# Short-conv adaLN layer in fp32: the turn of all tokens moved into the front as products with a diagonal of 1/rms

## The chip, the core and the metric

The kernel runs on one core of one Trainium2 chip. The metric is the device time of one execution in microseconds (us). The engines in this text are TensorE (PE, with its weight loads shown apart as PEld), VectorE (DVE), ScalarE (ACT) and the SyncE queue (SP), which issues nearly all of the DMAs. PSUM is the memory that PE writes; its tiles here come from two pools of buffers, "mm" (three buffers of two banks) and "sm" (two of one bank).

## The reference

One layer is computed for 256 tokens of width D = 2048, with inner width E = 4096:

```python
h = x / sqrt(mean(x*x) + eps) * g
shift, scale, gate = split(silu(c) @ ada_w + ada_b)     # ada_w is 2048 x 6144
h = h * (1 + scale) + shift
b, cg, v, gg = split(h @ w_in)                          # w_in is 2048 x 16384
u = causal_conv3(cg * v);  y = b * u * silu(gg)
x = x + gate * (y @ w_out);  out = rmsnorm(x, final_g)
```

All data are fp32. The weights are 128 MB (w_in), 48 MB (ada_w) and 32 MB (w_out), and each is read once.

## The kernel before, in words

A product with fp32 weights is made of three products in a faster format: `split` (L320) casts a piece of weights to `hi` on ACT (L324) and subtracts on DVE to get `lo` (L325), and PE multiplies hi by h's hi, hi by h's lo, and lo by h's hi (`product`, L419). Such a product needs h with the features on the partitions, so x is turned on PE first (`turn_x`, L281): ACT scales 512 columns of both token tiles by 1/rms (L285, L289), PE transposes them in blocks of 128 x 128 (L294), and ACT copies them out of PSUM into `xs` (L295). `modulate` (L300) then makes the hi and lo halves of `hT` for one pair of the 16 feature blocks, as soon as that pair's shift and scale are known.

Shift and scale come from ada_w. Two feature blocks at a time make a group: its 16 rows of blocks are multiplied by silu(c) and added up on DVE (`gv0` in the front, L348 and L350; `gv` later, L399 and L401), and PE or ACT adds over the partitions. In the front, three of the 16 blocks (7, 11, 15) are summed on PE instead (`sum0`, L337, products of one column), and a last such step adds `gv0`. So the front runs: load x (four DMAs), load ada_w's first columns (`at0`, twelve DMAs), square sums (ACT for token tile 0, L261; DVE for tile 1, L264), 1/rms (L270 to L272), the turn of the first 512 columns, the sums, `modulate(0, 2)`, first product. Between them, `idle(n)` (L238) puts n transposes of the identity on PE that nobody reads; the counts stand in `IDLE`. Everything of the front is pinned to the written order on each engine.

After the front, `plan()` lists steps: ("mm", ...) multiplies a chunk of 512 columns of w_in by the feature blocks that are ready, and ("ada", ...) loads one piece of a later group. An ada piece is two DMAs of 256 KB into one of four `at` buffers and two additions `gv` on DVE. A chunk's weights come as `raw_s`, 512 KB or 1 MB a DMA, in one of three `raw` buffers. The steps' order is fixed by the plan, but the order in which the pieces' instructions stand on SP, DVE and ACT is the scheduler's: it places them by priority and by its own estimate of when each could run. DVE works in its order: a `lo` behind a `gv` waits for that gv's DMA. The turns of the feature blocks 4 to 15 are put behind the 4th, 7th and 10th chunk (`LATER`, L486), with the turn of the convolution's taps (`rows2` into `cw`). SP's DMAs take eight semaphores in turn, so at most eight are under way, and a DMA into a buffer waits for DVE's last read of it.

After the "mm" chunks follow the second half of w_in (mm_b), the gates, and the product with w_out (mm_o).

Of the kernel before, what the change touches and what calls it, by code (L numbers as in the profile page):

```python
# [8 lines left out]
F32 = mybir.dt.float32  # L9
# [108 lines left out]
def short_conv_layer(ctx: ExitStack, tc: tile.TileContext, x, c, norm_g, ada_w, ada_b, w_in, conv_w, w_out, final_g, out):  # L118
# [69 lines left out]
    IDLE = (16, 30, 24, 14, 14, 6)  # L188
# [14 lines left out]
    for n, (j, kk) in enumerate(((0, 4), (4, 4), (8, 4), (12, 2), (14, 1), (15, 1))):  # L203
        at = wpool.tile([P, SLOT], F32, tag=("lo", "hi")[n % 2], name="at0", bufs=3)[:, : kk * 2 * NK0 * P]
        at = at.rearrange("p (k s f) -> p k s f", k=kk, s=2)
        if n == 0:
            wpool.tile([P, 32], F32, tag="line3", name="line3", bufs=1)
        if j == KT - 1:
            raw0 = raw_tile("raw0")
            first_load(raw0, 0)  # L210
        for s in range(2):
            nc.sync.dma_start(at[:, :, s, :], adas[:, j : j + kk, s, 0 : NK0 * P])  # L212
        first_ada.extend(at[:, i] for i in range(kk))
    for k in range(1, NK0):
        first_load(raw0, k)
# [20 lines left out]
    tp_idle = psum.tile([P, CT, T], F32, tag="mm", name="tp_idle")  # L236

    def idle(n):  # L238
        for _ in range(n):
            nc.tensor.transpose(tp_idle[:, 0, 0:P], ident, ident)  # L240

# [5 lines left out]
    idle(IDLE[0])  # L247
# [4 lines left out]
    idle(IDLE[1])  # L252
# [5 lines left out]
    for t in range(TT):  # L258
        for dh in range(2):
            if t == 0:  # L260
                sq = nc.scalar.activation(junk[:, t], xt[t][dh], AF.Square, accum_out=ssq[:, dh, t : t + 1])  # L261
                tc.add_manual_dep(sq.ins, root.ins.name, after, reason="one change of table")
            else:
                nc.vector.scalar_tensor_tensor(  # L264
                    out=junk[:, t], in0=xt[t][dh], scalar=1.0, in1=xt[t][dh], op0=ALU.mult, op1=ALU.mult,
                    accum_out=ssq[:, dh, t : t + 1],
                )
    nc.vector.tensor_copy(vec, tp_v)
    nc.vector.tensor_scalar_add(b_scale1, vec[:, 32:48], 1.0)
    nc.vector.tensor_tensor(out=rstd, in0=ssq[:, 0, :], in1=ssq[:, 1, :], op=ALU.add)  # L270
    nc.scalar.activation(rstd, rstd, AF.Sqrt, bias=eps_t, scale=1.0 / D)
    nc.vector.reciprocal(rstd, rstd)  # L272

# [5 lines left out]
    xs = [slot([P, CT, T], f"xs{j}") for j in range(KT // CT)]  # L279

    def turn_x(k0, k1, vector=False):  # L281

        c0, n = k0 % 8 * P, (k1 - k0) * P
        x0, x1 = (xt[t][k0 // 8][:, c0 : c0 + n] for t in range(TT))
        nc.scalar.activation(x0, x0, AF.Copy, scale=rstd[:, 0:1])  # L285
        if vector:
            nc.vector.tensor_scalar_mul(x1, x1, rstd[:, 1:2])
        else:
            nc.scalar.activation(x1, x1, AF.Copy, scale=rstd[:, 1:2])  # L289
        for i in range(0, k1 - k0, 2):  # L290
            tp = psum.tile([P, 2, T], F32, tag="sm", name="tp_x", bufs=2)
            for j in range(2):
                for t, xn in enumerate((x0, x1)):
                    nc.tensor.transpose(tp[:, j, t * P : (t + 1) * P], xn[:, (i + j) * P : (i + j + 1) * P], ident)  # L294
            nc.scalar.copy(xs[k0 // CT][:, k0 % CT + i : k0 % CT + i + 2, :], tp)  # L295
# [4 lines left out]
    def modulate(k0, nk, sums):  # L300

        ks = slice(k0, k0 + nk)
        if nk == 1:
            nc.vector.tensor_scalar(
                out=scale[:, ks], in0=sums[1], scalar1=b_scale1[:, ks], scalar2=gT[:, ks], op0=ALU.add, op1=ALU.mult
            )
            nc.scalar.activation(shift[:, ks], sums[0], AF.Identity, bias=b_shift[:, ks])
        else:
            nc.vector.tensor_tensor(out=scale[:, ks], in0=sums[1], in1=b_scale1[:, ks], op=ALU.add)
            nc.vector.tensor_tensor(out=scale[:, ks], in0=scale[:, ks], in1=gT[:, ks], op=ALU.mult)  # L310
            nc.vector.tensor_tensor(out=shift[:, ks], in0=sums[0], in1=b_shift[:, ks], op=ALU.add)
        for k in range(k0, k0 + nk):
# [19 lines left out]
    turn_x(0, 4)  # L332
# [8 lines left out]

    for k in range(KT):
        c_k = silu_c[:, k : k + 1]
        if k in ON_PE:
            idle(IDLE[2 + ON_PE.index(k)])
# [6 lines left out]
    pieces0 = [split(raw0[:, 0 : CT * P], CT * P)]  # L352
    modulate(0, NK0, (sums0[:, 0:NK0], sums0[:, NK0 : 2 * NK0]))
    idle(IDLE[-1])
# [131 lines left out]
    LATER = (4, 7, 10)  # L486
    whole = [0] * NCH
    for kind, *step in plan():
        if kind == "ada":
            ada_piece(*step)  # L490
        else:
            ch, k1 = step[0], step[3]
            part(*step)
            if step[2] == 0 and len(acc) in LATER:
                k = 4 + 4 * LATER.index(len(acc))
                with tc.issue_after(last_mm[0].ins), behind(ended):
                    turn_x(k, k + 4)
                    if k == 4:
                        turn(rows2, 0, 96, cw)
# [206 lines left out]
```

## Time and profile before

| what | us |
|---|---|
| time, median of 3 runs (all: 926.06, 925.84, 923.97) | 925.84 |
| span of the profiled execution | 925.9 |
| first product of the layer (L419) starts | 26.50 |
| PE's waits for `lo` behind it, three in number | 6.7 |
| PE busy in the span | 904.4 |
| DVE busy in the span | 613.9 |
| ACT busy in the span | 472.8 |

The profiled execution has no time of its own beside its span; 925.9 is within 0.1 us of the median. A row of the timeline gives start, duration, engine, line, operation, out<-in and the count of merged instructions, and in brackets the engine's idle time before it with what ended it. A row of windows gives, behind the stretch's bounds and length, the busy time and count for PE, PEld, DVE, ACT and POOL, then the granted PE clock (1.00 is full), the share of the DMA engines and GB/s. PE durations overlap, so the pace of a run of equal instructions is its length through its count.

### The profile page before, as it was taken

The page shows a single profiled execution, that of the slowest core. Times are in us where ns is not written, and L with a number is a line of the kernel's source. Part 1 is how long each engine was busy: PE and PEld are TensorE (multiplying, and loading weights), DVE is VectorE, ACT ScalarE, POOL GpSimd, SP SyncE. Part 2 cuts the span into 40 slices and gives each one's busy share as a digit, 9 for nine tenths or more (in the row PEclk, how much of TensorE's full clock was granted, in tenths as well). Part 3 has the DMA queues.
Part 4 walks back from the last instruction along what each step waited for, and adds up shares of the span by engine and source line. Part 5 has one row for each costly group of instructions (what it writes and reads, how often), then busy time and mean ns, then how long its engine had stood idle before and what let it go on. Part 6 is the DMA issues. An engine that isn't in the chain of part 4 may idle for free.

```text
span 925.9 us, 16464 instructions
## 1 busy us (share of the span) xinstructions
PE 904.4 (98%) x7119; PEld 869.6 (94%) x7119; DVE 613.9 (66%) x604; ACT 472.8 (51%) x465; POOL 0.7 (0%) x6
## 2 busy tenths in 40 slices
PE   7999899999999999999999999999999999999996
PEld 6999899999999999999999999999999988888885
DVE  5889888898486799875554455445554544545882
ACT  3787776675557856644434433443334433444333
POOL 0000000000000000000000000000000000000000
PEclk9999999999999999999999999999999999999999
DMA  9999999999895789776655665666556496566542
GB/s 314 355 367 355 367 329 338 350 365 358 268 306 186 219 297 357 243 231 201 202 186 188 199 204 184 189 199 204 183 183 195 140 348 226 186 200 205 182 137 92
DMA packets 163753, 227.66 MB, mean 246 GB/s; under 512 B 5680, under 2 KB 104160, under 8 KB 163296
## 3 DMA queue, kind: packets, MB, share of 16 engines
q1 hardware_dynamic: 163440, 226.51, 74.0%
q8 instruction: 56, 0.92, 0.4%
q14 instruction: 17, 0.14, 0.0%
q10 hardware_dynamic: 240, 0.09, 0.0%
HBM read 224.49 MB, written 2.10 MB: 245 GB/s over the span
## 4 chain that ended last, share of the span: by engine, by line
PE 88%; DMA 6%; DVE 3%; issue 1%; SPq 1%; ACT 1%; ACTq 0%; DVEq 0%
PE mm_b L419 38%; PE mm_s L419 31%; PE mm_o L604 6%; PE mm_o L605 6%; PE mm_o L603 6%; DMA at<-in_ada_w_dram 3%; DMA raw_s<-in_sc_w_in_dram 2%; DVE gv L401 1%; DVE lo L325 1%; DMA x<-in_x_dram 1%; SPq L212 0%; ACT hi L324 0%; PE ps_gate L542 0%; PE tp_g L408 0%; SPq L388 0%
## 5 line engine op out<-in xcount | busy, mean ns | idle before, releaser
L419 PE MATMUL mm_s<-hT,hi 128*128 128x256 f32 x2048 | 352.9, 278 | 0.1
L419 PE MATMUL mm_b<-hT,hi 128*128 128x256 f32 x2048 | 348.8, 276 | 0.0
L419 PEld LDWEIGHTS mm_s<-hT,hi 128*128 128x128 f32 x2048 | 310.4, 189 | 1.2 <-issue 0.5
L419 PEld LDWEIGHTS mm_b<-hT,hi 128*128 128x128 f32 x2048 | 308.4, 188 | 0.2 <-issue 0.2
L419 PE MATMUL mm_s<-hT,lo 128*128 128x256 f32 x1024 | 284.4, 279 | 6.8 <-DVE lo L325 6.7
L419 PE MATMUL mm_b<-hT,lo 128*128 128x256 f32 x1024 | 282.6, 276 | 0.0
L325 DVE TENSOR_TENSOR lo<-raw,hi 128x2048 fp32r<-128x2048 f32 (+1 forms) x66 | 148.1, 2244 | 135.1 <-ACT hi L324 135.1
L324 ACT CAST hi<-raw 128x2048 fp32r<-128x2048 f32 (+1 forms) x66 | 123.7, 1874 | 208.5 <-PE mm_b L419 150.2
L419 PEld LDWEIGHTS mm_s<-hT,lo 128*128 128x128 f32 x1024 | 193.1, 189 | 7.6 <-DVE lo L325 7.6
L419 PEld LDWEIGHTS mm_b<-hT,lo 128*128 128x128 f32 x1024 | 192.2, 188 | 0.2 <-issue 0.2
L325 DVE TENSOR_TENSOR lo<-raw_s,hi 128x2048 fp32r<-128x2048 f32 (+1 forms) x80 | 147.9, 1849 | 40.5 <-ACT hi L324 39.7
L324 ACT CAST hi<-raw_s 128x2048 fp32r<-128x2048 f32 (+1 forms) x80 | 124.6, 1557 | 67.6 <-PE mm_s L419 49.8
L325 DVE TENSOR_TENSOR lo<-raw_o,hi 128x2048 fp32r<-128x2048 f32 x32 | 73.3, 2291 | 65.1 <-ACT hi L324 65.0
L324 ACT CAST hi<-raw_o 128x2048 fp32r<-128x2048 f32 x32 | 61.0, 1907 | 107.2 <-PE mm_o L605 85.0
L604 PE MATMUL mm_o<-lo,y 128*128 128x512 f32 x256 | 99.7, 391 | 0.0
L603 PE MATMUL mm_o<-hi,y 128*128 128x512 f32 x256 | 99.3, 389 | 0.0
L605 PE MATMUL mm_o<-hi,y 128*128 128x512 f32 x256 | 99.3, 389 | 0.0
L401 DVE SCALAR_TENSOR_TENSOR gv<-at,silu_c,gv 128x512 f32<-128x512 f32 x105 | 78.6, 749 | 9.2 <-DMA at<-in_ada_w_dram 7.8
L440 ACT COPY acc<-mm_s 128x1024 f32<-128x1024 f32 x54 | 54.4, 1010 | 35.1 <-PE mm_s L419 34.9
L605 PEld LDWEIGHTS mm_o<-hi,y 128*128 128x128 f32 x256 | 48.0, 188 | 10.1 <-issue 0.2
L604 PEld LDWEIGHTS mm_o<-lo,y 128*128 128x128 f32 x256 | 48.0, 188 | 10.1 <-issue 0.2
L603 PEld LDWEIGHTS mm_o<-hi,y 128*128 128x128 f32 x256 | 48.0, 188 | 10.0
(94 smaller groups left out, 375.4 us busy)
## 6 DMA issues: line engine op xcount, KB each, us to landing
raw<-in_sc_w_in_dram SPq DMA_DIRECT2D x64, 1024.0 KB, 5.7
raw_s<-in_sc_w_in_dram SPq DMA_DIRECT2D x47, 1024.0 KB, 7.8
raw_o<-in_sc_w_out_dram SPq DMA_DIRECT2D x32, 1024.0 KB, 5.2
at<-in_ada_w_dram SPq DMA_DIRECT2D x114, 256.0 KB, 7.3
raw_s<-in_sc_w_in_dram SPq DMA_DIRECT2D x33, 512.0 KB, 5.8
at_g<-in_ada_w_dram SPq DMA_DIRECT2D x32, 512.0 KB, 8.0
at<-in_ada_w_dram SPq DMA_DIRECT2D x6, 512.0 KB, 8.8
x<-in_x_dram SPq DMA_DIRECT2D x4, 512.0 KB, 6.1
```

What stands on the lines that cost most here:

```text
L324: nc.scalar.copy(hi[:, :n], raw[:, :n])
L325: nc.vector.tensor_tensor(out=lo[:, :n], in0=raw[:, :n], in1=hi[:, :n].bitcast(F32), op=ALU.subtract)
L401: nc.vector.scalar_tensor_tensor(out=gv, in0=at4[:, i], scalar=c_k, in1=gv, op0=ALU.mult, op1=ALU.add)
L419: mm = last_mm[0] = nc.tensor.matmul(dst, w, h[:, k], start=begins and left, stop=ends, skip_group_check=True)
L440: nc.scalar.copy(acc[ch, q], bank)
L603: nc.tensor.matmul(po, yh, hi[:, o], start=opens, stop=False, skip_group_check=True)
L604: nc.tensor.matmul(po, yh, lo[:, o], start=False, stop=False, skip_group_check=True)
L605: nc.tensor.matmul(po, yl, hi[:, o], start=False, stop=ct == NCT - 1, skip_group_check=True)
```

## The change

All 16 feature blocks of both token tiles are turned in the front. No scaling of x on ACT and no transposes are left: a block of x is the stationary operand of a plain fp32 product, and the moving operand is `rooted`, the identity times 1/rms (128 x 128, made on DVE), so that the product both turns and scales. 1/rms is found for each token tile by itself (`root_of`): tile 0 by two squares on ACT, tile 1 by one on ACT and one on DVE. The results go into three "mm" buffers in PSUM, which ACT copies to `xs` 1024 columns at a time, and a fourth that takes the first one's buffer again. The turn of `rows2` moves into the front, between the two token tiles.

On SP the first half of the first weights (`raw0`) moves behind the last of `at0`. Of `gv0`'s blocks, five instead of three are summed on PE (7, 10, 11, 13, 15). The split of `raw0`'s first half on ACT and DVE moves behind shift and scale, within `modulate`. `IDLE` has 9 entries with other counts. Behind the front, the plan's steps are the same, without `LATER`.

```diff
-    IDLE = (16, 30, 24, 14, 14, 6)
+    IDLE = (16, 4, 4, 2, 8, 0, 0, 0, 5)
...
-        if j == KT - 1:
-            raw0 = raw_tile("raw0")
-            first_load(raw0, 0)
...
-    for k in range(1, NK0):
+    raw0 = raw_tile("raw0")
+    for k in range(NK0):
         first_load(raw0, k)
...
+    def root_of(t):
+        r = rstd[:, t : t + 1]
+        nc.vector.tensor_tensor(out=r, in0=ssq[:, 0, t : t + 1], in1=ssq[:, 1, t : t + 1], op=ALU.add)
+        nc.scalar.activation(r, r, AF.Sqrt, bias=eps_t, scale=1.0 / D)
+        nc.vector.reciprocal(r, r)
+        nc.vector.tensor_scalar_mul(rooted[:, t], ident, r)
+
+    def turn_x(tp, j, t):
+        for i in range(CT):
+            k = j * CT + i
+            nc.tensor.matmul(
+                tp[:, i, t * P : (t + 1) * P], xt[t][k // 8][:, k % 8 * P : (k % 8 + 1) * P], rooted[:, t],
+                start=True, stop=True, skip_group_check=True,
+            )
+
+    squares(0, 0, False)
+    squares(0, 1, False)
+    root_of(0)
+    nc.vector.tensor_copy(vec, tp_v)
+    nc.vector.tensor_scalar_add(b_scale1, vec[:, 32:48], 1.0)
+    for j in range(3):
+        turn_x(turned[j], j, 0)
+    turn(rows2, 0, 96, cw)
+    squares(1, 0, False)
+    squares(1, 1, True)
+    root_of(1)
+    idle(IDLE[2], turned[2])
+    for j in range(3):
+        turn_x(turned[j], j, 1)
+        nc.scalar.copy(xs[j], turned[j])
...
-    ON_PE = (7, 11, 15)
+    ON_PE = (7, 10, 11, 13, 15)
...
-    LATER = (4, 7, 10)
...
-            if step[2] == 0 and len(acc) in LATER:
-                k = 4 + 4 * LATER.index(len(acc))
-                with tc.issue_after(last_mm[0].ins), behind(ended):
-                    turn_x(k, k + 4)
-                    if k == 4:
-                        turn(rows2, 0, 96, cw)
```

The order on three places. First DVE in the front, before, from the square sums to the first of `gv0` (x10 and x11 are the halves of token tile 1, at0_96 the first piece of ada_w):

```order
L264 SCALAR_TENSOR_TENSOR junk_187,ssq_185<-x10_86 128x1024
L264 SCALAR_TENSOR_TENSOR junk_187,ssq_185<-x11_87 128x1024
L268 COPY vec_127<-tp_v_152 128x64
L269 TENSOR_SCALAR b_scale1_154<-vec_127 128x16
L270 TENSOR_TENSOR rstd_186<-ssq_185 128x2
L272 RECIPROCAL rstd_186<-rstd_186 128x2
L348 TENSOR_SCALAR gv0_205<-at0_96,silu_c_129 128x512
```

The same stretch of DVE with the change:

```order
L273 TENSOR_TENSOR rstd_162<-ssq_161 128x1
L275 RECIPROCAL rstd_162<-rstd_162 128x1
L276 TENSOR_SCALAR rooted_169<-ident_118,rstd_162 128x128
L289 COPY vec_127<-tp_v_154 128x64
L290 TENSOR_SCALAR b_scale1_156<-vec_127 128x16
L230 COPY cw_128<-tp_v_190 128x96
L263 SCALAR_TENSOR_TENSOR junk_163,ssq_161<-x11_87 128x1024
L273 TENSOR_TENSOR rstd_162<-ssq_161 128x1
L275 RECIPROCAL rstd_162<-rstd_162 128x1
L276 TENSOR_SCALAR rooted_169<-ident_118,rstd_162 128x128
L361 TENSOR_SCALAR gv0_221<-at0_96,silu_c_129 128x512
```

The copy of `cw`, which waits for PE's turn of `rows2`, now stands ahead of the squares of x11, and with them ahead of the second root and of all of `gv0`.

Second, PE in the front, before, from the turn's end to the layer's first product (tp_idle are the transposes that nobody reads):

```order
L240 MATMUL tp_idle<-ident 128x128 x24
L337 MATMUL sum_204<-silu_c,at_100 128x1 x4
L240 MATMUL tp_idle<-ident 128x128 x14
L337 MATMUL sum_204<-silu_c,at_103 128x1 x4
L240 MATMUL tp_idle<-ident 128x128 x14
L337 MATMUL sum_204<-silu_c,at_112 128x1 x4
L337 MATMUL sum_204<-ones,gv_205 128x1 x4
L240 MATMUL tp_idle<-ident 128x128 x6
```

The same stretch of PE with the change, from the products of token tile 1 on (x_86 and x_87 are its halves, x_85 is the second half of tile 0):

```order
L281 MATMUL tp_x<-rooted,x_86 128x128 x8
L281 MATMUL tp_x<-rooted,x_87 128x128 x4
L281 MATMUL tp_x<-rooted,x_85 128x128 x4
L281 MATMUL tp_x<-rooted,x_87 128x128 x4
L238 MATMUL tp_idle<-ident 128x128 x2
L347 MATMUL sum_220<-silu_c,at_100 128x1 x4
L238 MATMUL tp_idle<-ident 128x128 x8
L347 MATMUL sum_220<-silu_c,at_103 128x1 x8
L347 MATMUL sum_220<-silu_c,at_106 128x1 x4
L347 MATMUL sum_220<-silu_c,at_112 128x1 x4
L347 MATMUL sum_220<-ones,gv_221 128x1 x4
L238 MATMUL tp_idle<-ident 128x128 x5
```

Ahead of the sums now stand 20 products of token tile 1 and of the last 512 columns, and between the last four sums no transposes.

Third, DVE some 70 us behind the front, before, from the 20th to the 21st `lo` of raw_s (at_1593, at_1685 and at_1690 are the 25th to 27th ada piece; on SP, raw_s_1255 is issued ahead of at_1690):

```order
L325 TENSOR_TENSOR lo_1225<-raw_s_1222,hi_1224 128x1024
L401 SCALAR_TENSOR_TENSOR gv_1592<-at_1593,silu_c_129,gv_1592 128x512
L401 SCALAR_TENSOR_TENSOR gv_1592<-at_1685,silu_c_129,gv_1592 128x512 x2
L401 SCALAR_TENSOR_TENSOR gv_1592<-at_1690,silu_c_129,gv_1592 128x512 x2
L325 TENSOR_TENSOR lo_1258<-raw_s_1255,hi_1257 128x2048
```

The same two `lo` with the change (at_1442, at_1524 and at_1616 are the 24th to 26th piece; on SP, raw_s_1186 is issued ahead of at_1616):

```order
L334 TENSOR_TENSOR lo_1156<-raw_s_1153,hi_1155 128x1024
L413 SCALAR_TENSOR_TENSOR gv_1145<-at_1442,silu_c_129,gv_1145 128x512
L413 SCALAR_TENSOR_TENSOR gv_1523<-at_1524,silu_c_129,gv_1523 128x512
L413 SCALAR_TENSOR_TENSOR gv_1145<-at_1442,silu_c_129,gv_1145 128x512
L413 SCALAR_TENSOR_TENSOR gv_1523<-at_1616,silu_c_129,gv_1523 128x512
L334 TENSOR_TENSOR lo_1189<-raw_s_1186,hi_1188 128x2048
```

The 21st `lo` now stands behind one addition of the 26th piece, where it stood behind both additions of the 27th.

More of the change, by code (lines that the diff above doesn't have):

```diff
@@ L233, in turn, with idle @@
         return tp
-    tp_idle = psum.tile([P, CT, T], F32, tag="mm", name="tp_idle")
-    def idle(n):
+    turned = [psum.tile([P, CT, T], F32, tag="mm", name="tp_x") for _ in range(3)]
+    def idle(n, where):
         for _ in range(n):
-            nc.tensor.transpose(tp_idle[:, 0, 0:P], ident, ident)
+            nc.tensor.transpose(where[:, CT - 1, P:T], ident, ident)
     warm = const.tile([P, 1], F32, tag="warm", name="warm")
@@ L257, in short_conv_layer @@
     junk = hpool.tile([P, TT, HX], F32, tag="big", name="junk")
[L258 to L272, printed above, removed]
     hT = hpool.tile([P, KT, 2 * T], F32R, tag="big", name="hT")
@@ L279, in short_conv_layer, with squares @@
     xs = [slot([P, CT, T], f"xs{j}") for j in range(KT // CT)]
[L281 to L285, printed above, removed]
+    rooted = slot([P, TT, P], "rooted")
+    def squares(t, dh, vector):
         if vector:
-            nc.vector.tensor_scalar_mul(x1, x1, rstd[:, 1:2])
-        else:
[L289 to L295, printed above, removed]
+            nc.vector.scalar_tensor_tensor(
+                out=junk[:, 1], in0=xt[t][dh], scalar=1.0, in1=xt[t][dh], op0=ALU.mult, op1=ALU.mult,
+                accum_out=ssq[:, dh, t : t + 1],
+            )
+        else:
+            sq = nc.scalar.activation(junk[:, 0], xt[t][dh], AF.Square, accum_out=ssq[:, dh, t : t + 1])
+            tc.add_manual_dep(sq.ins, root.ins.name, after, reason="one change of table")
@@ L311, in modulate @@
             nc.vector.tensor_tensor(out=shift[:, ks], in0=sums[0], in1=b_shift[:, ks], op=ALU.add)
+        if between:
+            between()
         for k in range(k0, k0 + nk):
@@ L340, in sum0 @@
             )
+    for t in range(TT):
+        turn_x(last_turned, 3, t)
+    nc.scalar.copy(xs[3], last_turned)
     for k in range(KT):
@@ L344, in short_conv_layer @@
         if k in ON_PE:
-            idle(IDLE[2 + ON_PE.index(k)])
+            idle(IDLE[3 + ON_PE.index(k)], tp_idle)
             sum0(k, first_ada[k], c_k)
```

16 lines of the change are left out of this document (9 added, 7 removed).

## The prediction

> **What bounds the kernel now.** I read the page's head first, then the windows on both sides of the last long wait, then who waited for whom.
>
> ```profile
> span 925.9 us, 16464 instructions
> 26.50:105.90 79.40, 72.56 (x616) 71.53 (x616) 72.32 (x96) 63.06 (x86) 0.00 (x0) 0.99 1.07 362
> 105.90:925.90 820.00, 812.50 (x6358) 780.24 (x6358) 527.83 (x481) 400.58 (x365) 0.00 (x0) 1.00 0.71 232
> PE mm_s L419 <- DVE lo L325: 6.7, 3, 3.7
> ```
>
> From 105.9 us on, PE is busy for 812.5 of 820 us: that stretch is bound by PE, and nothing in the change touches its work. Between the first product (26.50) and 105.9, PE is idle for 79.40 - 72.56 = 6.8 us, which is the three waits for `lo`, while the DMA engines are full all the time (share 1.07 at 362 GB/s). So this stretch is bound by what has been loaded, and the end of the kernel hangs on the moment when the last of the three waits, the one of 3.7 us, is over. What PE does before it costs nothing unless it moves that moment. The timeline of DVE shows what it is made of:
>
> ```profile
> 96.42 1.23 DVE L325 TENSOR_TENSOR lo<-raw_s,hi 128x1024 fp32r<-128x1024 f32 x1
> 97.55 2.33 DVE L401 SCALAR_TENSOR_TENSOR gv<-at,silu_c,gv 128x512 f32<-128x512 f32 x3
> 102.10 1.54 DVE L401 SCALAR_TENSOR_TENSOR gv<-at,silu_c,gv 128x512 f32<-128x512 f32 x2 [2.22 <-DMA at<-in_ada_w_dram]
> 103.55 2.28 DVE L325 TENSOR_TENSOR lo<-raw_s,hi 128x2048 fp32r<-128x2048 f32 x1
> ...
> 106.00:108.00 2.00, 2.00 (x15) 2.00 (x16) 1.61 (x4) 1.91 (x4) 0.00 (x0) 0.82 1.10 353
> 108.00:110.00 2.00, 2.00 (x11) 2.00 (x11) 2.00 (x1) 0.93 (x1) 0.00 (x0) 0.50 1.10 355
> 110.00:112.00 2.00, 2.00 (x17) 2.00 (x16) 1.51 (x3) 1.25 (x3) 0.00 (x0) 0.82 1.04 380
> ```
>
> The 21st `lo` (103.55, ends 105.83) stands behind two `gv` of the 27th ada piece, which landed at 102.1. After the wait, PE's granted clock falls to 0.50: 0.18 x 2 + 0.50 x 2 + 0.18 x 2 = 1.7 us of full-speed work are lost there, in the stretch that PE bounds.
>
> **The turns taken out of the stream.** Gone behind the front are 24 transposes on PE, 12 scalings on ACT and 6 copies.
>
> ```profile
> 28.30 0.72 ACT L285 ACTIVATE x<-x,rstd 128x512 f32<-128x512 f32 x1
> L295 ACT COPY xs<-tp_x x8: 585/592/606, 14.5 to 59.9; 128x512 f32<-128x512 f32 x8
> 8.65 3.49 PE L240 MATMUL tp_idle<-ident 128*128 128x128 f32 x30
> ```
>
> A transpose costs PE 3.49 / 30 = 0.116 us, so 24 x 0.116 = 2.8 us of PE, and ACT saves 12 x 0.72 + 6 x 0.59 = 12.2 us. The last of these copies starts at 59.9, before the wait of 102: all of it lies where PE has 6.8 us to spare, so I price it at 0. PE comes to the wait earlier and waits longer. If that cover were gone, it would be -2.8 us.
>
> **The front.** These rows carry it, in order of time.
>
> ```profile
> 4.32 3.67 PE L240 MATMUL tp_idle<-ident 128*128 128x128 f32 x16
> 8.16 0.19 ACT L261 ACTIVATION_READ_ACCUMULATOR junk<-x 128x1 f32 x1
> 10.37 1.22 DVE L264 SCALAR_TENSOR_TENSOR junk<-x 128x1024 f32<-128x1024 f32 x1 [0.22 <-DMA x<-in_x_dram]
> 11.52 0.08 DVE L264 DVE_READ_ACCUMULATOR junk<-x 128x1 f32 x1
> 11.52 0.22 DVE L268 COPY vec<-tp_v 128x64 f32<-128x64 f32 x1
> 11.86 0.15 DVE L270 TENSOR_TENSOR rstd<-ssq 128x2 f32<-128x2 f32 x1
> 12.38 0.17 DVE L272 RECIPROCAL rstd<-rstd 128x2 f32<-128x2 f32 x1 [0.36 <-ACT rstd L271]
> 13.40 0.49 DVE L348 TENSOR_SCALAR gv<-at,silu_c 128x512 f32<-128x512 f32 x1 [0.86 <-DMA at<-in_ada_w_dram]
> 17.40 0.95 PE L337 MATMUL sum<-silu_c,at 128*128 128x1 f32 x8
> 19.43 4.69 DVE L350 SCALAR_TENSOR_TENSOR gv<-at,silu_c,gv 128x512 f32<-128x512 f32 x6 [0.69 <-DMA at<-in_ada_w_dram]
> 23.34 1.05 PE L337 MATMUL sum<-silu_c,at 128*128 128x1 f32 x8 [1.03 <-DMA at<-in_ada_w_dram]
> 25.33 0.16 DVE L309 TENSOR_TENSOR scale<-sum,b_scale 128x2 f32<-128x2 f32 x1 [0.60 <-PE sum L337]
> 26.48 0.41 DVE L315 TENSOR_SCALAR xs<-xs,scale,shift 128x256 f32<-128x256 f32 x1 [0.73 <-ACT hT L314]
> 686.52 0.86 PE ps_gate L542 x2
> ```
>
> Price of a turning product: the trace has no fp32 product of 128 columns. An fp32 product shows as two instructions (8 for the 4 of a sum). With one column they cost 0.95 / 8 = 0.119 us each, which is the weight load's pace; with 512 columns 0.86 / 2 = 0.43, so 128 columns are 0.107. Side by side: 0.119 an instruction, 0.24 a product; one behind the other: 0.119 + 0.107 = 0.226, 0.45 a product. I take 0.24, because the stream's 616 products in 72.56 us, 0.118 each, leave no room for loads in a row with them.
>
> Token tile 0: squares done at 8.35; the root takes 12.55 - 11.86 = 0.69, the diagonal about 0.27 (between the 0.22 for 64 columns and the 0.41 for 256): 9.4. Twelve products x 0.24 = 2.9: 12.3. Then PE turns `rows2`, and DVE, in its order, waits for that with the copy of `cw` (about 0.25) before it may square x11, which landed by 10.37. The wait is new, and behind it on DVE stand the second root and all of `gv0`. So: 12.9, squares 1.3, root 0.69, diagonal 0.27: 15.2 us. From there PE: 20 products x 0.24 = 4.8, 10 transposes x 0.116 = 1.2, five sums and the last at 0.96 each = 5.8: 27.0 us, against 25.3 before (the wait of L309). PE is the chain: `gv0` starts 15.2 instead of 13.40, but has 11 of 13 additions, so it ends at 15.2 + 0.4 + 10 x 0.78 = 23.4 (before 24.1), and the last `at0`, some 0.7 us sooner without 256 KB ahead of it, is there at 22.6 where PE asks at 25.1. What the loads' order and the two extra sums were to save is hidden behind PE. The front is 1.7 us later: first product at 28.2.
>
> The clock adds to that. At half clock from a point on, a stretch of 2 us shows 0.84 if the point is 0.64 us before its end: the falls of the trace are at 25.4 (below) and, from the 0.82 above, at 107.3.
>
> ```profile
> 22.00:24.00 2.00, 0.97 (x9) 0.73 (x7) 1.93 (x3) 0.62 (x1) 0.00 (x0) 1.00 1.04 344
> 24.00:26.00 2.00, 2.00 (x17) 2.00 (x17) 1.11 (x5) 0.15 (x1) 0.00 (x0) 0.84 0.91 322
> 26.00:28.00 2.00, 1.98 (x10) 1.58 (x9) 1.45 (x4) 2.00 (x4) 0.00 (x0) 0.50 1.07 358
> 28.00:30.00 2.00, 2.00 (x16) 2.00 (x16) 1.89 (x4) 2.00 (x4) 0.00 (x0) 0.80 1.10 354
> ...
> 68.00:70.00 2.00, 1.09 (x8) 0.69 (x6) 1.96 (x2) 2.00 (x4) 0.00 (x0) 1.00 1.06 382
> 70.00:72.00 2.00, 0.95 (x8) 0.95 (x9) 2.00 (x4) 0.47 (x1) 0.00 (x0) 1.00 1.07 366
> ```
>
> The first lasted 0.64 + 2.0 + 0.8 = 3.4 us and came although sums ran from 23.3 to 25.3: products of one column seem to count for little. PE's idle 0.9 + 1.05 us around 70 made no fall. With the change, PE runs nothing but these from 22.2 to 27.0. A fall within that doubles the price of the sums left: 0 to 2.9 us, by where it comes; I take 1.2. The Trainium skill ("TensorE: Matmul & The Clock Gate", Part 1) says that the clock is judged in windows of about 3.4 us that run free of the kernel; 81.9 us between the two falls is 24 such windows, so the trace agrees.
>
> **What the front does to the loads.** The first raw buffer comes free with the second `lo` of raw0:
>
> ```profile
> 28.05 0.68 DVE L325 TENSOR_TENSOR lo<-raw,hi 128x512 fp32r<-128x512 f32 x1
> 28.77 2.09 SPq L462 DMA_DIRECT2D raw_s<-in_sc_w_in_dram x2
> 36.00 1.06 ACT L324 CAST hi<-raw_s 128x1024 fp32r<-128x1024 f32 x1 [0.21 <-DMA raw_s<-in_sc_w_in_dram]
> DMA to landing us min/median/max: 3.5/7.1/11.3
> at<-in_ada_w_dram SPq DMA_DIRECT2D x114, 256.0 KB, 7.3
> ```
>
> The second of that pair was issued by 30.86 and landed at 36.0, 5.1 us later; the shortest way of a raw_s is 3.5. So the queue holds 1.6 us here. A front that is 1.7 + 1.2 = 2.9 us late runs it dry for about 1.3 (0.1 at full clock, 3.0 at worst), and since the DMA engines bound the stretch, that time is lost: +1.3.
>
> **The order of the loads further on.** With the change, the 21st `lo` waits for the first addition of the 26th piece. One piece is 2 x 256 KB, 1.45 us at 362 GB/s, and one addition is 0.77: 2.2 us sooner. More, up to 3.0, if the 26th piece lands with the raw weights ahead of it. DVE had 2.22 us to spare ahead of it, so its own work lets about as much through. I take -2.4.
>
> **The sum.** -2.4 + 1.3 = -1.1 for the end of the last wait. The wait is then still some 2 to 3 us long, so the fall of the clock behind it is likely but not sure, and a part of its 1.7 us may fall into the wait: -0.5. That makes 925.9 - 1.6 = 924.3, and on the scale of the runs, whose median is 0.1 lower, 924.2 us.
>
> **The rivals.** The faster one: the front keeps its clock (the loads slip by 0.1) and the shorter wait lets no fall follow. Then -2.3 - 1.7 = -4.0, 921.8; with half of a slip 923.0. For it: the 2 us of idle PE around 70 let the clock stand. Against it: in the front 4.8 us of one-column products.
>
> The slower one: the turning products pay load and pass one behind the other, 0.226 an instruction. Then 24 instructions before the copy of `cw` and 40 behind it cost 64 x 0.107 = 6.8 us more, the first product comes at 35 us, the loads slip by 1.7 + 6.8 - 1.6 = 6.9, and the end moves by +4.5: 930.4. It decides from where the slip passes 2.4, so a front 4.0 us late, which 64 instructions reach at 0.155 us each. Against it: the stream's 0.118 a product, with a load for every one.
>
> The third: transposes don't hold the clock up. Then PE's last real work in the front ends at 20.0, the fall may come as early as a fall lasts, 3.4 us, behind that, at 23.4, the 3.6 us of sums left double, the first product comes at 31.8 and the loads slip by 3.7, of which the order gives back 2.4, and the changed fall 0.5: 926.7. The trace speaks against it: 16 transposes from 4.32 ran at 0.229 us each and the 30 from 8.65 at 0.116, with no product between. The Trainium skill ("TensorE: Matmul & The Clock Gate", Part 4) states this very thing, that transposes don't count as busy for the clock; by the rows here it does not hold.
>
> That the change does not do what it says has a case too: the turns do leave the stream, yet with the 2.8 us priced at nothing, the time stays within a microsecond; that lies within my forecast.
>
> **How the numbers follow.** Forecast 924.2 with 0.48 (923.0 to 925.9), the faster case 0.28, the third 0.10 (around 926.7), the slower 0.14 (928 to 931). A measurement of this kernel can tell 0.3%, 2.8 us, from no change: below 923.1 lie the faster case and 0.06 of the forecast, 0.34; above 928.6 most of the slower case, 0.12; between them 0.54. The range 921.4 to 927.2 leaves out the slower case and a little of the faster.
>
> **What would show it.** Right: `gv0` starts near 15.2, not 13.4; `scale` of the front waits for PE's sums until 27 or later; the first product at 28 to 31; turning products at 0.12 an instruction; the 21st `lo` ends near 104.7 and PE waits for it; no product waits behind it. Wrong: a first product at or before 26.5; a last wait somewhere else, above all behind 110; no wait at all near 104, which would make the 2.8 us count.

## The result, and the profile with the change

The changed kernel takes 930.58 us (median of 6 runs, 928.53 to 932.75), the kernel before 925.23 beside it (6 runs, 923.97 to 926.06): a ratio of 1.0058, 95% interval 1.0046 to 1.0070. It is slower by 5.4 us, where 1.6 us faster was forecast, and it lies outside the forecast range of 921.4 to 927.2.

One correction to the scale comes first. Every profiled execution from here on has a time of its own, and it lies 1.8 us above the span (931.7 and 929.9 here). So the profiled execution of before, with its span of 925.9, was one of 927.7 us, near the slow end of what that kernel does (923.67 to 928.18 in 25 runs), and not one of the median, as the prediction took it.

The head of the page with the change, and the windows on both sides of the last wait for a `lo` (length, then busy time of PE, PEld, DVE, ACT, POOL, granted clock, DMA share, GB/s):

```profile
span 929.9 us, 16416 instructions
```

```profile
32.98:111.69 78.71, 73.77 (x590) 72.50 (x590) 69.96 (x93) 53.58 (x68) 0.00 (x0) 0.93 0.96 324
111.69:929.90 818.21, 810.63 (x6358) 778.42 (x6358) 529.76 (x484) 402.02 (x371) 0.00 (x0) 1.00 0.71 235
```

The second row is the old one (6358 matmuls, PE busy all the time) without its fall of the clock. The loss lies ahead of it: the first product at 32.98 instead of 26.50, and a DMA share of 0.96 instead of 1.07 in the stretch that hangs on the loads. The front in the timeline, then windows of the front and of the stretch behind it, with the clock and the DMA engines:

```profile
9.55 4.81 PE L281 MATMUL tp_x<-rooted,x 128*128 128x128 f32 x24
14.48 0.26 DVE L230 COPY cw<-tp_v 128x96 f32<-128x96 f32 x1 [4.69 <-PE tp_v L228]
17.05 6.30 PE L281 MATMUL tp_x<-rooted,x 128*128 128x128 f32 x40 [2.16 <-DVE rooted L276]
25.12 4.94 PE L347 MATMUL sum<-silu_c,at 128*128 128x1 f32 x32
29.92 1.84 PE L347 MATMUL sum<-ones,gv 128*128 128x1 f32 x8
32.98 1.22 PE L431 MATMUL mm_s<-hT,hi 128*128 128x256 f32 x4
35.25 1.90 SPq L474 DMA_DIRECT2D raw_s<-in_sc_w_in_dram  x2
```

```profile
16.00:18.00 2.00, 0.95 (x4) 0.95 (x5) 1.57 (x5) 0.29 (x1) 0.00 (x0) 0.74 1.10 351
18.00:20.00 2.00, 2.00 (x12) 2.00 (x11) 1.89 (x4) 0.84 (x1) 0.00 (x0) 0.50 1.09 347
...
28.00:30.00 2.00, 2.00 (x11) 2.00 (x11) 0.00 (x0) 0.00 (x0) 0.00 (x0) 0.50 1.10 351
30.00:32.00 2.00, 2.00 (x11) 2.00 (x11) 0.16 (x1) 0.00 (x0) 0.00 (x0) 0.50 0.58 187
32.00:34.00 2.00, 1.96 (x10) 1.56 (x9) 1.83 (x6) 1.67 (x4) 0.00 (x0) 0.50 0.04 12
34.00:36.00 2.00, 2.00 (x11) 2.00 (x11) 1.97 (x5) 0.93 (x2) 0.00 (x0) 0.50 0.00 0
36.00:38.00 2.00, 2.00 (x13) 2.00 (x13) 2.00 (x3) 0.99 (x1) 0.00 (x0) 0.64 0.75 224
38.00:40.00 2.00, 2.00 (x20) 2.00 (x19) 1.97 (x3) 1.66 (x2) 0.00 (x0) 1.00 0.67 172
...
94.00:96.00 2.00, 2.00 (x19) 1.84 (x17) 2.00 (x3) 2.00 (x3) 0.00 (x0) 1.00 0.50 130
96.00:98.00 2.00, 1.69 (x15) 1.65 (x14) 1.97 (x4) 2.00 (x3) 0.00 (x0) 1.00 0.85 248
```

DVE waits 4.69 us for PE's turn of `rows2` before it may copy `cw`; the second root comes behind that, and PE in its turn waits 2.16 us for `rooted`. The pace shows the clock: 4.81 / 24 = 0.20 us an instruction for tile 0. (The granted clock reads 1.00 there, as it does over the first 16 transposes, which take 3.67 / 16 = 0.229 us each; so this half clock is read from the pace alone, against the 2.94 us that the same 24 instructions take in other executions below.) The 40 instructions behind PE's wait began at half clock (the rows at 16 and 18), and the last of the six one-column sums ran at 0.50 of the clock. The first raw buffer comes free at 35.25, 6.5 us later than before (28.77), and by then every load in the queue has landed: from 30 to 40 us the DMA engines lose 2 x (0.42 + 0.96 + 1.00 + 0.25 + 0.33) = 5.9 us, where before lost none. Later they lose another 2.2: 1.3 at 94 to 98 and 0.9 at 52 to 58.

PE waits for the 21st `lo` until 111.69, 5.8 us later than before:

```profile
111.69 0.39 PE L431 MATMUL mm_s<-hT,lo 128*128 128x256 f32 x1 [0.95 <-DVE lo L334]
```

This wait is only 0.95 us long. From its first product to the end of the wait PE is idle for no more than 78.71 - 73.77 = 4.9 us, at a mean clock of 0.93: late and partly at half clock, PE is itself not far from being the limit of this stretch.

### The profile page after: what moved, and what is told of

It is laid out like the page before. It is cut to its first block, busy times and chain, and to the rows that moved or that the text cites. A ratio compares the mean times of both kernels' runs of the same rounds, so it can differ in the third digit from the quotient of the medians.

```text
span 929.9 us, 16416 instructions
## 1 busy us (share of the span) xinstructions
PE 910.7 (98%) x7102; PEld 875.9 (94%) x7102; DVE 611.7 (66%) x604; ACT 467.7 (50%) x456; POOL 0.7 (0%) x6
## 4 chain that ended last, share of the span: by engine, by line
PE 89%; DMA 5%; DVE 3%; issue 1%; ACT 0%; ACTq 0%; SPq 0%; DVEq 0%
PE mm_b L431 37%; PE mm_s L431 30%; PE mm_o L608 6%; PE mm_o L609 6%; PE mm_o L610 6%; DMA at<-in_ada_w_dram 3%; DVE lo L334 1%; DVE gv L413 1%; PE tp_x L281 1%; DMA raw_s<-in_sc_w_in_dram 1%; PE sum L347 1%; DMA rows<-in_ada_b_dram 1%; PE ps_gate L547 0%; PE tp_g L420 0%; DVE xs L324 0%
```

## The experiments

Theory T1: a front that is late by more than the load queue holds lets the DMA engines run dry, and the last wait slips by what they lose; the front is late through the wait of `cw`, the five sums and the half clock. Rival T2: the new order of the loads in the stream makes the time by itself, whatever the front does. Runs of the changed kernel can't part the two cleanly: a moved step or another count in `IDLE` also changes the scheduler's estimate, and with it the order of the loads behind the front. "Idle DMA" below is the sum of 2 x (1 - share) over the windows of 2 us from 10 to 106 us in which the share is under 1: 0.2 us before, 8.2 with the change.

### A late front without the change

```diff
-    IDLE = (16, 30, 24, 14, 14, 6)      # the kernel before
+    IDLE = (16, 30, 24, 14, 74, 6)
```

> The kernel before, with one number changed: 74 instead of 14 idle transposes ahead of the last of its three sums of the front, so its front is 60 x 0.109 = 6.5 us late at the full clock, as late as the change made it, while the turns of x stay in the stream as they were. T1 (a front that is late by more than the load queue holds runs the DMA engines dry, and the last wait slips by the remainder): first product near 33.0 instead of 26.5, the DMA engines idle for some 5 us between 30 and 40, the last lo of the loading stretch about 4 to 6 us late, less the 2 us that the changed order of this lo gives (it falls behind the 26th piece here, as in the change): 925.2 + 2 to + 6, so 927 to 931. T2 (the new order of the loads in the stream makes the time, the front does not): within 1 us of 925.2. The view that PE's waits of 6.8 us hide a late front gives the same, within 1 us.

Measured: 930.53 us, ratio 1.0061 (1.0044 to 1.0078) to before: the change's time within 0.1 us, with the turns still in the stream and no turning product. The first product came at 31.99, the last wait ended at 111.60, idle DMA 5.3. The windows of this run show the same hole as the change, although the clock is full:

```profile
30.00:32.00 2.00, 1.50 (x14) 1.27 (x14) 0.42 (x4) 0.66 (x2) 0.00 (x0) 1.00 0.86 277
32.00:34.00 2.00, 2.00 (x17) 1.94 (x17) 1.93 (x5) 2.00 (x4) 0.00 (x0) 1.00 0.11 31
34.00:36.00 2.00, 1.66 (x12) 1.43 (x12) 2.00 (x4) 2.00 (x4) 0.00 (x0) 1.00 0.36 46
36.00:38.00 2.00, 2.00 (x18) 2.00 (x18) 1.93 (x3) 2.00 (x4) 0.00 (x0) 1.00 0.73 242
38.00:40.00 2.00, 1.10 (x9) 0.75 (x7) 1.97 (x3) 2.00 (x3) 0.00 (x0) 1.00 0.77 233
```

4.3 of the 5.3 us of idle DMA lie at 28 to 40, and behind the front, up to 105 us, at most two ada pieces stand between two raw loads, as before. So a late front is enough for a loss as large as the change's, and PE's waits in the stream do not hide it. (The profiled execution was the slowest of the four, 933.16: behind its last wait the clock falls, to 0.77 at 112 to 114 and 0.50 at 114 to 116.) The second kernel is the same with 39 instead of 74:

> The kernel before with 39 instead of 14 idle transposes at the same place: its front is 25 x 0.109 = 2.7 us late. T1 (only what goes beyond the 1.6 us that the load queue holds is lost): first product near 29.2, DMA engines idle for about 1.1 us, and with the order of the last lo changed by -2 the time is 925.2 - 1.5 to + 1.5. If a late front were paid in full, without cover: + 2.7, 927.9. T2: within 1 us of 925.2, which this run alone can't tell from T1.

Measured: 925.63 us, ratio 1.0016 (1.0006 to 1.0026), first product 27.98, so 1.5 us late and not 2.7, idle DMA 1.8 (0.5 of it at 32 to 36). A front 1.5 us late costs 0.9 to 1.5 us, by the medians and by the ratio, and one 5.5 us late 5.6 to 5.8. The queue's cover of 1.6 us is there (the share stays at 1.03 until 32), but the loss is somewhat more than lateness less cover: when the loads start again, as the last two rows show, they run at shares of 0.73 and 0.77 for 4 us, which is 1.0 us lost besides.

### The wait of `cw` taken out

```diff
-    turn(rows2, 0, 96, cw)                  # between the two token tiles
...
+    turn(rows2, 0, 96, cw)                  # behind the additions of gv0
     sum0(None, gv0, ones[:, 0:1])
```

> The changed kernel with one step moved: the turn of rows2 and the copy of cw stand behind the additions of gv0 and not ahead of the squares of x11. T1: DVE no longer waits for PE's turn at 12.2 to 14.5, so root(1) ends near 12.7 instead of 16.7, the second tile's products start about 4 us sooner, the first product comes at 25.5 to 28 and not at 33, the DMA engines are idle between 30 and 40 for less than 1 us, and the time is 921 to 925. T2 (the loads' order in the stream): the dips of DMA at 52 to 58 and 94 to 98 stay, 929 to 931. If the five one-column sums alone hold the front up, root(1) comes sooner but the first product stays at 31 or later: 927 to 930.

Measured: 925.93 us, ratio 1.0017 (1.0007 to 1.0027). Against the kernel before, timed beside each, the loss goes from 5.4 to 1.2 us (1.6 by the ratio). Its timeline and windows:

```profile
12.33 0.28 DVE L276 TENSOR_SCALAR rooted<-ident,rstd 128x128 f32<-128x128 f32 x1
14.01 4.63 PE L281 MATMUL tp_x<-rooted,x 128*128 128x128 f32 x40
20.42 4.90 PE L346 MATMUL sum<-silu_c,at 128*128 128x1 f32 x32
28.35 1.22 PE L431 MATMUL mm_s<-hT,hi 128*128 128x256 f32 x4
```

```profile
28.00:30.00 2.00, 1.96 (x9) 1.66 (x8) 1.80 (x6) 2.00 (x4) 0.00 (x0) 0.50 1.10 349
30.00:32.00 2.00, 2.00 (x11) 2.00 (x11) 2.00 (x3) 0.93 (x2) 0.00 (x0) 0.50 0.80 228
```

The second diagonal is ready at 12.6 instead of 17.0. All five sums are still there and the clock is half from 22.5 to 32.8, and the front is 1.9 us late; idle DMA is 0.6. That fits T1. It doesn't refute T2 by itself, since the order of the loads moved with the step: three ada pieces now stand between two raw loads at 35, 43 and 53 us, and the four at 85 to 92 of the change are gone. The expected 921 to 925 was too low by 1 us: the gain over the kernel before that I counted on does not come.

Next, four sums and more idle transposes besides:

```diff
-    IDLE = (16, 4, 4, 2, 8, 0, 0, 0, 5)
+    IDLE = (16, 4, 0, 2, 12, 4, 4, 6)
...
-    ON_PE = (7, 10, 11, 13, 15)
+    ON_PE = (7, 11, 13, 15)
```

> The run with cw behind the sums, and besides that four sums on TensorE instead of five, with a few more idle transposes ahead of them (12, 4, 4, 6). T1: one sum of 0.96 us less in PE's chain and no fall of the clock in the front: first product 25.5 to 26.5, no idle DMA, 921 to 923.5. T2: 929 to 931. If one-column sums don't matter, the same as the run with five.

Measured: 925.58 us, ratio 1.0005 (0.9993 to 1.0017). The first product came at 26.13, as expected, with full clock from 8.4 to 25.4 us, and the time is still that of before, 2.1 us above the 923.5 at which my expectation ended. With no lateness left, 24 transposes, 6 scalings and 6 copies fewer in the stream are worth nothing that can be measured in this kernel, which has a hole of 1.7 us in its loads (below).

### The clock alone, and the sums alone

Both keep the wait of `cw`:

```diff
-    IDLE = (16, 4, 4, 2, 8, 0, 0, 0, 5)     # the change
+    IDLE = (16, 4, 24, 2, 8, 8, 8, 8, 5)    # first kernel
...
+    IDLE = (16, 4, 4, 2, 8, 0, 5)           # second kernel
+    ON_PE = (7, 11, 15)
```

> The changed kernel with more idle transposes and nothing else: 24 instead of 4 in PE's wait between the two token tiles, 8 ahead of each of the four sums that had 8, 0, 0 and 0. The wait of cw, the five sums and the order on SP stay as in the change. T1 with the half clock as the largest part of the late front: no half clock behind 9 us, tile 0 turned by 12.5, root(1) by 15.1, then 40 instructions 4.5, six sums 5.8 and 24 transposes 2.6: first product near 29.5 instead of 33.0 although PE has 2.6 us more to do; DMA engines idle for 1 to 2 us between 30 and 40, the dip at 94 to 98 stays, 926 to 928. If the half clock is not what makes the front late (the chain of waits and sums is): the transposes only add, first product at 33 or later, 930 or more. T2 (the order on SP, which is the same here): 930.

> The changed kernel with three sums on TensorE (7, 11, 15), as before the change, and the wait of cw left in. T1: two sums fewer in PE's chain at half clock, 2 to 3 us: first product at 30 to 31, DMA engines idle for 2 to 3.5 us between 30 and 40, 926.5 to 929. If the wait of cw alone sets the front: first product at 32 to 33, 930.

Measured: 929.71 us, ratio 1.0052 (1.0037 to 1.0067), and 930.42 us, 1.0050 (1.0033 to 1.0067). Both missed what was expected, on the slow side: neither takes back more than 1 us for certain. Yet in the profile of the first the front did what it should: the first product came at 29.72 with 2.6 us more for PE to do, and no half clock between 8 and 28. It was the fastest of its four executions (927.4), so a second profile was taken, below.

The profile of the second kernel (an execution of 928.99 us) goes against T1 as the whole account:

```profile
27.97 1.22 PE L431 MATMUL mm_s<-hT,hi 128*128 128x256 f32 x4
109.72 0.38 PE L431 MATMUL mm_s<-hT,hi 128*128 128x256 f32 x1 [1.20 <-ACT hT L323]
110.35 0.58 PE L431 MATMUL mm_s<-hT,lo 128*128 128x256 f32 x1 [0.25 <-DVE lo L334]
```

With the wait of `cw` in, but with tile 0 and the 40 instructions at full clock (2.94 and 4.73 us) and two sums fewer, the first product came at 27.97. That is 2 us sooner than the 30 to 31 expected, and sooner than in the run with `cw` moved (28.35). The DMA engines were idle for 1.5 us only, and still this execution took 3.6 us more than the kernel before (925.42) and the median 5.0 more. Its last waits are for `hT` on ACT and the `lo` behind it, at the end of another order. So a front 1.5 us late can go with a loss of this size too, and T1 does not explain this run.

The first kernel a second time:

> The run with more idle transposes alone, profiled a second time. Its median of 929.7 missed what was expected (926 to 928), while its profiled execution, the fastest of its four, had 927.4, a full clock from 8.1 and a first product at 29.7. If the place of the clock's windows is what differs between executions: where this execution takes 929 us or more, its full clock comes at 11 to 14, its first product at 31 or later, and the DMA engines are idle for over 4 us at 28 to 40; where it takes 927 to 928, full clock at 8 to 9, first product near 29.7. If the executions differ by the loads alone: first product near 29.7 and about 3 us of idle DMA whatever the time.

Measured: 928.86 us, with the front as in its first profile, so the windows' place is not what differed there:

```profile
29.90 1.23 PE L431 MATMUL mm_s<-hT,hi 128*128 128x256 f32 x4 [0.43 <-ACT hT L323]
```

```profile
30.00:32.00 2.00, 2.00 (x10) 2.00 (x11) 1.93 (x5) 1.80 (x3) 0.00 (x0) 0.50 0.74 236
32.00:34.00 2.00, 2.00 (x17) 2.00 (x17) 2.00 (x4) 1.06 (x1) 0.00 (x0) 0.90 0.37 60
34.00:36.00 2.00, 2.00 (x20) 2.00 (x19) 2.00 (x3) 1.02 (x1) 0.00 (x0) 1.00 0.88 259
36.00:38.00 2.00, 2.00 (x20) 2.00 (x20) 1.75 (x3) 1.05 (x1) 0.00 (x0) 1.00 0.82 235
```

A front that is 3.4 us late at full clock still loses 2 x (0.26 + 0.63 + 0.12 + 0.18) = 2.4 us, and the order of the loads, which puts four ada pieces in one place as the change does, another 1.3 at 90 to 94 (shares of 0.81 and 0.56). With the wait of `cw` in, filling PE's idle time does not bring the front back, because 2.6 of the 3.4 us are the added transposes themselves. For the same reason this run does not show how large a part of the loss the clock alone makes.

### The order of the loads

Between the 18th and the 19th raw load the change puts four ada pieces on SP (eight DMAs); before had one or two between any two raw loads there. This is the hole at 94 to 98:

```profile
84.59 0.37 SPq L474 DMA_DIRECT2D raw_s<-in_sc_w_in_dram  x1
85.26 6.91 SPq L400 DMA_DIRECT2D at<-in_ada_w_dram  x8
94.57 0.37 SPq L474 DMA_DIRECT2D raw_s<-in_sc_w_in_dram  x1
```

The 19th raw load waits for a buffer, and so for a `lo` that stands behind additions on DVE. The run with four sums has such a hole too (shares of 0.83, 0.67 and 0.66 at 84 to 90). Two kernels with as good a front, in which the scheduler's order comes out even, test what that costs:

```diff
-    IDLE = (16, 4, 0, 2, 12, 4, 4, 6)       # the run with four sums
+    IDLE = (16, 8, 0, 4, 12, 6, 6, 6)       # first kernel
...
+    IDLE = (16, 8, 0, 2, 12, 8, 6)          # second kernel
+    ON_PE = (7, 11, 15)
```

> As the run with cw behind the sums and four sums (925.6 us), with 4, 2, 2 and 2 more idle transposes: the front is the same to half a microsecond, but the scheduler, to whose estimate these count, spreads the loads evenly: between two raw loads of the 4th to 21st stand one or two ada pieces, where that run had up to three at six places. Theory: in that run the front is no longer late, and what is left is the hole in the DMA engines at 84 to 90 (shares 0.83, 0.67, 0.66: 1.7 us), made by the bunched order; here it is gone, idle DMA under 0.6 us from 10 to 106, and the time is 922 to 924.3. Rival: the order makes no difference, because the stretch hangs on the bytes and on DVE's additions alone: 924.8 to 926, as in that run.

> As the run with the even order, but with three sums on TensorE (7, 11, 15) instead of four; the loads are as evenly spread. Theory: first product 0.5 to 1 us sooner or the same (DVE has one addition of 0.77 more), which the load queue hides: the same as the run with the even order within 0.7 us, 922 to 924.3. Rival (the order makes no difference): 924.8 to 926.

Measured: 928.77 us, ratio 1.0035 (1.0019 to 1.0051), and 926.24 us, 1.0012 (1.0003 to 1.0021). The holes are gone in both (idle DMA 0.2 and 0.0), the first products come at 26.27 and 26.43, and neither kernel is faster. The theory of the hole falls as an account of what is left, and the waits of PE show why. The first kernel's:

```profile
105.48 0.39 PE L431 MATMUL mm_s<-hT,lo 128*128 128x256 f32 x1 [0.54 <-DVE lo L333]
110.09 0.38 PE L431 MATMUL mm_s<-hT,hi 128*128 128x256 f32 x1 [1.20 <-ACT hT L322]
110.72 0.39 PE L431 MATMUL mm_s<-hT,lo 128*128 128x256 f32 x1 [0.25 <-DVE lo L333]
```

The same place in the second kernel's, where a wait for `lo` follows and ends at 108.32:

```profile
107.69 0.38 PE L431 MATMUL mm_s<-hT,hi 128*128 128x256 f32 x1 [0.92 <-ACT hT L322]
```

Another wait took the place of the one that came earlier: a later pair of feature blocks is not ready, since ACT works without a pause from 98.5 us on with casts and copies ahead of it, and the last wait ends at 110.72 and 108.32. The spans, 926.2 and 923.7, differ by as much as these two moments, 2.5 and 2.4 us. In the profiles of both kernels before and with the change no product waits for `hT`; in the run with three sums one does. So an order can cost time by itself: the first kernel loses 3.4 us to the kernel before with its front on time and its DMA engines full. The first was profiled again, since its times spread from 926.2 to 931.2:

> The run with the even order, profiled a second time. Its first profile had no hole in the DMA engines, a last wait that ended at 105.5 and a time of 928.0; its other times went from 926.2 to 931.2. If the clock in the front is what makes the spread, this profile shows a first product later than 26.3 with a hole in the DMA engines at 28 to 36 where its time is above 929, and one at 26.3 with a last wait near 105 where it is below 927. If the loads run at different speed by themselves, first product 26.3 and no hole, whatever the time.

Measured: 927.25 us, first product 26.42, last waits at 104.85, 109.46 (`hT`) and 110.09, idle DMA 0.5. It repeats the first profile to 0.6 us, so the wait for `hT` belongs to this order. What its executions of 929 to 931 us do differently, neither profile shows.

### Both kernels a second time

> The kernel before, profiled a second time. The times of one kernel differ by 3 to 5 us from execution to execution, and the profiled execution of before (a span of 925.9, and times lie 1.8 above spans, so 927.7) stands about 3 us above the median of its times, 924.7 to 925.4. If what differs is where the windows of the clock fall, this one shows its falls elsewhere: a span of 922 to 924.5 with no half clock behind the last wait, and the last lo of the loading stretch within 1 us of 105.8. If it is the loads, that lo ends 1.5 to 3 us sooner.

> The changed kernel, profiled a second time. In the first profile the clock was full from 13.5 and half again for 3.4 us at 17.0 and for 10.2 at 27.2. If the windows' place decides the front: a first product at 29 to 32 instead of 33.0 where the full clock comes at 8 to 9, the DMA engines idle for 2.5 to 5 us at 30 to 40 instead of 5.9, and a span between 926 and 930, in step. If the half clock follows from the kernel's own idle stretches: first product at 32.5 to 33.5 again.

Before: 923.42 us, and a span of 921.6. The DVE around the last wait, and PE behind it:

```profile
97.00 3.89 DVE L401 SCALAR_TENSOR_TENSOR gv<-at,silu_c,gv 128x512 f32<-128x512 f32 x5
100.81 2.28 DVE L325 TENSOR_TENSOR lo<-raw_s,hi 128x2048 fp32r<-128x2048 f32 x1
103.15 0.39 PE L419 MATMUL mm_s<-hT,lo 128*128 128x256 f32 x1 [1.21 <-DVE lo L325]
```

```profile
26.61:103.15 76.54, 72.59 (x616) 71.52 (x616) 72.53 (x96) 61.35 (x83) 0.00 (x0) 0.98 1.07 365
103.15:921.60 818.45, 810.88 (x6358) 778.63 (x6358) 527.99 (x481) 401.99 (x368) 0.00 (x0) 1.00 0.71 234
```

The five additions run without a pause. The 2.22 us that DVE waited for the 27th ada piece in the first profile are not there, nor is the fall of the clock behind the last wait: 105.89 - 103.15 = 2.7 us of wait and 1.6 us of clock (820.00 less 818.45) make the 4.3 us between the two spans. Neither belongs to every execution. The fall came again in the profiles with 74 and with 39 idle transposes, each of them the slowest execution of its kernel.

The cast that this `lo` reads ended 0.4 us before it:

```profile
98.54 1.91 ACT L324 CAST hi<-raw_s 128x2048 fp32r<-128x2048 f32 x1
```

So here an earlier place in DVE's order could have let the `lo` start at 98.54 + 1.91 = 100.45 instead of 100.81, and no sooner. The chain that ends in this wait lies on DVE alone from 85 us on. The loads bound the last wait in the first profile (the piece landed at 102.1) and in both profiles of the change (DVE waits 0.86 and 1.26 us for the 26th piece just ahead of the `lo`), but not in this one.

With the change: 931.27 us, and a span of 929.5.

```profile
9.50 2.94 PE L281 MATMUL tp_x<-rooted,x 128*128 128x128 f32 x24 [0.26 <-DVE rooted L276]
12.56 0.26 DVE L230 COPY cw<-tp_v 128x96 f32<-128x96 f32 x1 [2.78 <-PE tp_v L228]
14.79 0.29 DVE L276 TENSOR_SCALAR rooted<-ident,rstd 128x128 f32<-128x128 f32 x1
15.13 6.31 PE L281 MATMUL tp_x<-rooted,x 128*128 128x128 f32 x40 [2.16 <-DVE rooted L276]
31.06 1.22 PE L431 MATMUL mm_s<-hT,hi 128*128 128x256 f32 x4
```

Tile 0 ran at full clock this time (2.94 us instead of 4.81), so the first product came 1.9 us sooner, as expected. The time did not move in step, as I had expected too: the span is only 0.4 us shorter and the last wait ends only 0.3 sooner. And the 40 instructions behind PE's wait took 6.31 us again (4.73 at full clock in the run with the clock alone), and the sums ran at half clock from 25.3 us again. So when the clock becomes full decides 1.9 us of the front, and the half clock among the sums came in both. The half clock behind PE's wait came in both too, but not in the profile of the run with three sums, which has the same wait of 2.16 us and the 40 instructions in 4.73. Idle DMA is 7.0 (4.0 of it at 30 to 38, 2.5 at 52 to 58 and 92 to 96), and the last wait ends at 111.40, 8.2 us behind the second profile of before. Idle DMA is 6.8 us more than there; where the other 1.4 went is open.

## Why the prediction was wrong, point by point

- **The bound** was right: in all four profiles of the two kernels, 818 us of PE work follow on the last wait (820.0 with a fall of the clock, 818.45, 818.21, 818.10), and the time goes with the moment at which that wait ends. That the loads set this moment holds for the profile it was read from and for the change, but not for the second profile of before, where DVE's own work set it.
- **The turns taken out of the stream**, priced at 0: nothing speaks against it. With the front mended, 925.58 us against 924.74 (1.0005, 0.9993 to 1.0017), in one kernel with an order of its own. The 12 scalings are 6, though: two in each of the three turns behind the front, all started between 28.3 and 31.4. ACT saves 6 x 0.72 + 6 x 0.59 = 7.9 us, not 12.2; the sum does not use it.
- **The price of a turning product**, 0.12 us an instruction: right (2.94 / 24 = 0.12). The slower rival's 0.226 does not occur at full clock; its time, 930.4, was met by another mechanism, so it was not borne out.
- **The chain up to the second root** was right at full clock: `cw` at 12.3 to 12.9 forecast and 12.56 measured, the diagonal at 15.2 forecast and 14.79 + 0.29 = 15.1 measured. In the other profile the half clock under tile 0 made it 17.0.
- **The clock in the front** is the first step that failed: 1.2 us, with 2.9 as the upper end. Against the 28.2 without any half clock, the first product was 2.9 us later in one profile (31.06) and 4.8 in the other (32.98). I looked for a fall only among the last sums. It may also lie under tile 0, and it came, in both profiles, behind PE's new wait of 2.16 us for the second diagonal, a wait that I had in my own chain (12.9 to 15.2) and did not weigh for the clock. With it the front was 4.5 to 6.5 us late and not 2.9, and the slip of the loads, +1.3 in the sum, became 4.0 to 5.9.
- **The cover of the load queue**, 1.6 us, was about right, but starting the loads again costs about 1 us besides, so a front 4.5 to 6.5 us late loses 4.0 to 5.9 us of DMA and not the 2.9 to 4.9 that lateness less cover gives.
- **The order of the loads**, -2.4, is the second step that failed. It stood on the 2.22 us that DVE waited in one execution; the second profile of before has no such wait, and there at most 0.4 us were to be gained. The new order has holes of 2.2 to 2.5 us instead. That these were paid in full is not shown: two kernels without holes, in orders of their own, were no faster. The row was real, but it was one draw.
- **The fall behind the last wait**, -0.5: against the one profile of before that has it, the change did save it (818.1 to 818.2 us behind the wait, not 820.0); against the other there was nothing to gain.
- **The faster rival** did not come: the front lost its clock, and the last wait became later. One of its sums is wrong besides: half of a slip of 1.3 - 0.1 = 1.2 us is 0.6, which makes 922.4 and not 923.0.
- **The third rival**, that transposes do not hold the clock up, was not the mechanism, though its half clock among the sums came. The run with the clock alone had nothing but transposes, one-column sums and turning products on PE, and it shows no half clock between 9 and 28 us in either profile. The Trainium skill ("TensorE: Matmul & The Clock Gate", Part 4) says that transposes don't count as busy in the same way; no run here bears that out.

Set right, the sum is: 4.0 to 5.9 us of idle DMA behind the late front and 2.2 to 2.5 in holes, 6.5 to 8.1 in all, against no gain. This adds up idle time and does not prove each part. The last wait moved by 5.8 us from first profile to first, which is about 8.1 less the 2.2 that before lost in its first profile, and by 8.2 from second to second; the medians moved by 5.4.

What the edits of the front were worth, against the kernel before timed beside each: with `cw` moved the loss is 1.2 us instead of 5.4, with the clock filled alone 4.3, with two sums fewer alone 5.0, the last two within what their intervals leave open. These are not prices of the parts, since each edit came with an order of its own. What is shown is that a front as late as the change's is enough for the loss; how the loss divides between the late front and the order is open. None of the kernels run beat the kernel before.

## What to carry to other kernels

When a step is moved forward into an engine's fixed order, name everything that stands behind its wait on that engine, and price the worst clock under each stretch that the chain runs through: here one copy of 0.26 us, put where its input came late, held up the squares, the root, the other engine's products and in the end the loads. Where loads bound a stretch, as here, a late start was free only for about the 1.6 us that the queue still held; beyond that it cost its lateness and about 1 us of restart. Where a scheduler chooses the order, compare the orders of two kernels before their times: with a front on time, one order cost 3.4 us. Before a term of 2 us is built on one wait or one fall of the clock, a second profile of the same kernel must show it too.

## What the hardware showed that was not expected

- With the same instructions ahead of them, tile 0's 24 instructions took 4.81 us in one execution of the changed kernel and 2.94 in the other. The Trainium skill ("TensorE: Matmul & The Clock Gate", Part 1) says that the ramp differs from run to run with the place of the free-running window; these two profiles agree. It calls the cost of the ramp less than 1% of a usual span; here it was 1.9 us, 0.2%, in the front, of which 0.4 reached the span.
- A wait of 2.16 us on PE was followed by a half clock of 3.4 us in both profiles of the change and by none in the run with three sums, so a wait of this length is a risk to the clock and not a rule.
- Executions of one kernel differ by 2 to 5 us (923.67 to 928.18 for before in 25 runs). Two profiles of before differ by 4.3 us in span, of which one late DMA explains 2.7 and one fall of the clock 1.6.
